# Narrow projections packed side by side, a row turned by one-row products, and a store moved to later

## The chip, the cores and the metric

The kernel runs on one core of a Trainium2 chip. The metric is device time in microseconds (us) of one execution. TensorE (PE in the rows; PEld is its weight load) multiplies, VectorE (DVE) and ScalarE (ACT) do elementwise work, GpSimd (POOL) a few small operations, and SyncE (SP) issues most transfers.

## The reference, cut to what matters

The model has two layers over 1024 tokens of width 1024. The change touches the start of layer 0 and its three small projections:

```python
mod = c_act @ ada_w[l] + ada_b[l]                 # (1, 1024) @ (1024, 6*1024)
sh1, sc1, g1, sh2, sc2, g2 = jnp.split(mod, 6, axis=-1)
h = modulate(rms_norm(x, norm1[l]), sh1, sc1)     # h * (1 + sc1) + sh1
...
xx = jnp.pad(h, ((0, 0), (1, 0), (0, 0)))[:, :-1] - h
xw = h + xx * mu[1]; xk = h + xx * mu[2]; xv = h + xx * mu[3]
xa = h + xx * mu[4]; xg = h + xx * mu[5]; xr = h + xx * mu[0]
r, k, v = xr @ w_rkv[0], xk @ w_rkv[1], xv @ w_rkv[2]
w = -softplus(-(w0 + tanh(xw @ w1) @ w2)) - 0.5   # w1: 1024 x 64
a = sigmoid(a0 + (xa @ a1) @ a2)                  # a1: 1024 x 64
g = sigmoid(xg @ g1) @ g2                         # g1: 1024 x 160
```

After these come a recurrent scan over the tokens (the wkv stage), an output projection, a feed-forward block, and a second layer with differential attention and another feed-forward block. All inputs are float32.

## The kernel before

Activations are held transposed: 128 features on the partitions, 512 tokens (half of the sequence) along the row. A width of 1024 is thus eight blocks, counted by k.

The kernel is written as generators that yield now and then, and `merge` and hand-written counters interleave them as the program is emitted. A scheduler then orders the instructions of each engine: it takes the ready instruction that stands earliest in the program, ready by its own model of the chip's times. Each engine runs that fixed order, and so does each queue that issues transfers. What stands earlier in the program thus tends to be issued earlier, but not always.

The start goes as follows. `tm_fetch(0)` loads the first half of x in four pieces (`xt`). `ada_pe` loads the first 2048 columns of the modulation weight in eight pieces of 1 MB (`adw`), and multiplies each with the column of activated conditioning as it lands (L260): four matmuls of one output row each, which write to PSUM partitions 0, 32, 64 and 96. `tm_load(0)` transposes x on TensorE (L353), copies each block to a tile `xs` (three buffers), and stores it in DRAM as `x_d` from ScalarE's queue (L356), where it is read much later; it also squares x for the norm (L349) and scales x (L361). When the modulation product is done, ScalarE copies its four rows to SBUF (L264), four transfers fold them into 16 rows of 128 (L267), one TensorE transpose turns these into 16 columns (L269), and L271 adds the bias: this is `mod`, the shift and the scale. `tm_norm(0)` then transposes the scaled x again (L375) and writes h, with scale and shift, alternately on VectorE (L379) and ScalarE (L377).

`tm_proj(0)` comes next. It loads w1, a1 and g1 (L399 to L401), and for each k makes three mixes of h with its shifted self, `xw`, `xa` and `xg` (each one ScalarE instruction, L388, and one VectorE instruction, L389), and multiplies: w1 (64 columns) into partitions 0 to 63 of the bank b1 (L408), a1 (64 columns) into partitions 64 to 127 of b1 (L410), the first 128 columns of g1 into b2 (L412), and its last 32 into b3 (L413). All three mixes share one tag with two buffers. The results are put through tanh (L417, L420), adjusted (L421) and stored as `lora_d` (L423). The second part of `tm_proj` is the three wide projections, 24 blocks each of 24 matmuls (L109 to L111) over mixes split in two parts (L100, L101); its buffers lie where those of the first part lay.

The generator `rest` is merged into `tm_proj(0)`: the transposes, squares and h of the second half of x, then the other modulation columns, summed on VectorE (`ada_ve`, L281 and L283) and turned into columns by products with ones (L290). `tm_proj(1)`, the same for the second half of the tokens, runs later beside the first tiles of the wkv stage.

Of the kernel before, what the change touches and what calls it, by code (L numbers as in the profile page):

```python
# [9 lines left out]
F32 = mybir.dt.float32  # L10
# [7 lines left out]
P = 128  # L18
# [67 lines left out]
class Trunk:  # L86
# [155 lines left out]
    def ada_pe(self, l, c0):  # L242

        nc, tc, A = self.nc, self.tc, self.A
        with self.pool("ad", ADB, "right") as ad:
            ws = []

            def fetch(n):
                for k in range(len(ws), min(n, NK)):
                    w = ad.tile([P, 2048], F32, tag="adw", name="adw")  # L250
                    nc.sync.dma_start(w, A["ada_w"][l][k * P:(k + 1) * P, c0:c0 + 2048])
                    ws.append(w)
            fetch(ADB)
            yield
            ps = self.pm.tile([P, HS], F32, tag="m", name="adps")
            for k in range(NK):
                fetch(k + 1)
                w = ws[k]
                for n in range(4):
                    nc.tensor.matmul(ps[32 * n:32 * n + 1, :], self.ca[:, k:k + 1], w[:, n * HS:(n + 1) * HS],  # L260
                                     start=(k == 0), stop=(k == NK - 1))
            row = ad.tile([P, HS], F32, tag="adrow", name="adrow", bufs=1)
            for n in range(4):
                nc.scalar.copy(row[32 * n:32 * n + 1, :], ps[32 * n:32 * n + 1, :])  # L264
            rt = ad.tile([16, P], F32, tag="adrt", name="adrt", bufs=1)
            for n in range(4):
                nc.sync.dma_start(rt[4 * n:4 * n + 4, :], row[32 * n:32 * n + 1, :])  # L267
            tp = self.pm.tile([P, HS], F32, tag="m", name="adtp")
            nc.tensor.transpose(tp[:, :16], rt, self.ident[:16, :16])  # L269
            q = c0 // P  # L270
            nc.vector.tensor_tensor(out=self.mod[l][:, q:q + 16], in0=tp[:, :16], in1=self.adab[l][:, q:q + 16], op=ALU.add)  # L271
# [71 lines left out]
    def tm_load(self, half, xn, nx):  # L343
# [6 lines left out]
        for k in range(NK):  # L350
            tp = self.pm.tile([P, HS], F32, tag="m", name="tp")
            for q in range(4):
                nc.tensor.transpose(tp[:, q * P:(q + 1) * P], xn[q][:, k * P:(k + 1) * P], self.ident)  # L353
            xs = nx.tile([P, HS], F32, tag="xs", name="xs", bufs=3)
            (nc.scalar.copy if k % 2 else nc.vector.tensor_copy)(xs, tp)
            nc.scalar.dma_start(self.x_d[half, k], xs)  # L356
            yield
# [25 lines left out]
    def mix(self, half, m, k, pool):  # L383
# [3 lines left out]
        xm = pool.tile([P, HS], F32, tag="xm", name="xm")  # L387
# [5 lines left out]
    def tm_proj(self, half):  # L393
        nc, tc, A = self.nc, self.tc, self.A
        with self.pool("lo") as lo, self.pool("lt", 2) as lt:
# [5 lines left out]
            nc.sync.dma_start(g1, A["a_g1"][0].rearrange("(k p) f -> p k f", p=P))  # L401
            b1 = self.pm.tile([P, HS], F32, tag="m", name="b1")
            b2 = self.pm.tile([P, HS], F32, tag="m", name="b2")
            b3 = self.pm.tile([P, HS], F32, tag="m", name="b3")
            for k in range(NK):
                f, l = k == 0, k == NK - 1
                xw = self.mix(half, 1, k, lt)
                nc.tensor.matmul(b1[0:64, :], w1[:, k, :], xw, start=f, stop=l)  # L408
                xa = self.mix(half, 4, k, lt)
                nc.tensor.matmul(b1[64:128, :], a1[:, k, :], xa, start=f, stop=l)  # L410
                xg = self.mix(half, 5, k, lt)
                nc.tensor.matmul(b2, g1[:, k, 0:128], xg, start=f, stop=l)  # L412
                nc.tensor.matmul(b3[0:32, :], g1[:, k, 128:160], xg, start=f, stop=l)  # L413
# [5 lines left out]
            for gl, b in ((r[2], b2), (r[3][0:32], b3[0:32, :])):  # L419
# [1295 lines left out]
def trunk(ctx, tc, A, out):  # L1715
# [9 lines left out]
    next(ada)  # L1725
    xn.append(t.tm_fetch(1, nx))
    drain(t.tm_load(0, xn[0], nx))
    drain(ada)
    t.gamma(0, 0)

# [16 lines left out]
    merge(t.tm_proj(0), side, NSA, False)  # L1747
# [151 lines left out]
```

## Time and profile before

| | us |
|---|---|
| three runs | 3251.70, 3259.11, 3259.45 |
| median of the runs | 3259.11 |
| the profiled execution's own time | 3252.99 |
| its span in the trace | 3251.2 |
| TensorE's mean granted clock in it | 0.952 of full |

The profiled execution lies 6 us under the median. In the rows below, a line such as L260 is that of the kernel before. A timeline row gives the start, the busy time, the engine, the line, the operation, what it writes and reads, the number of instructions merged into the row, and in brackets how long the engine sat idle before it and what ended that. A float32 matmul shows as two MATMUL records, each with its own weight load.

### The profile page before, as it was taken

To read this page: it belongs to the slowest core of one execution; us is meant where nothing else is said; L and a number is where in the kernel's file an instruction comes from. 1 tells how busy PE (TensorE), PEld (TensorE's weight loads), DVE (VectorE), ACT (ScalarE), POOL (GpSimd) and SP (SyncE) were. 2 spreads that over 40 slices of the span, in tenths; PEclk is the share of its full clock that TensorE was granted. 3 is DMA by queue.
4 is the path that set the end of the run, shared out by engine and by line. 5 is a ranking of instruction groups with operands and counts; after the bars stand their busy time and mean duration, and the time that the engine had idled before them with its cause. 6 is when DMAs were issued, how large, how long until landed. Compare 5 with 4: busy or idle time off the path is not lost.

```text
span 3251.2 us, 53634 instructions
## 1 busy us (share of the span) xinstructions
PE 2984.1 (92%) x21607; PEld 2400.7 (74%) x21607; DVE 2154.7 (66%) x3824; ACT 1231.3 (38%) x2189; POOL 95.1 (3%) x74
## 2 busy tenths in 40 slices
PE   5998888988899989999999789899899999999997
PEld 2574667877677767888887678778677888888885
DVE  2656877657787766777778486876667555555555
ACT  3544555565555443222223243444333212222123
POOL 0000000110000000000000000000000000000000
PEclk7999989988899999999999899999899999999998
DMA  7363334344333366455443544545552111111111
GB/s 245 114 207 112 110 106 136 103 117 136 114 118 106 101 194 209 141 171 156 141 123 127 162 122 125 151 134 155 143 192 71 52 46 41 58 52 46 39 46 52
DMA packets 441403, 387.86 MB, mean 119 GB/s; under 512 B 42832, under 2 KB 369856, under 8 KB 440130
## 3 DMA queue, kind: packets, MB, share of 16 engines
q1 hardware_dynamic: 438850, 380.23, 38.8%
q8 instruction: 170, 2.79, 0.4%
q10 hardware_dynamic: 2304, 4.20, 0.3%
q14 instruction: 79, 0.65, 0.1%
HBM read 298.74 MB, written 83.49 MB: 118 GB/s over the span
## 4 chain that ended last, share of the span: by engine, by line
PE 57%; DVE 9%; issue 5%; DMA 2%; ACT 2%; POOL 0%; SPq 0%; DVEq 0%; POOLq 0%; ACTq 0%
PE u L109 9%; PE u L111 9%; PE u L110 9%; PE d L109 5%; PE d L111 5%; PE d L110 5%; PE ps L109 3%; PE ps L110 3%; PE ps L111 3%; PE sc L1577 1%; PE tp L1504 1%; PE sc L1578 1%; DVE mx L1582 1%; DVE pd L1596 1%; DMA wraw<-in_ffn_w_up_dram 1%
## 5 line engine op out<-in xcount | busy, mean ns | idle before, releaser
L109 PE MATMUL u<-h,whl 128*128 128x512 f32 x1408 | 562.8, 400 | 5.3 <-ACT whl L163 3.8
L110 PE MATMUL u<-h,whl 128*128 128x512 f32 x1408 | 554.4, 394 | 2.4 <-DVE whl L164 2.4
L111 PE MATMUL u<-h,whl 128*128 128x512 f32 x1408 | 553.5, 393 | 1.3 <-DVE h L1129 1.3
L1172 DVE SCALAR_TENSOR_TENSOR x<-d,mod,x 128x512 f32<-128x512 f32 x352 | 261.9, 749 | 180.9 <-PE d L111 180.8
L109 PEld LDWEIGHTS u<-h,whl 128*128 128x128 f32 x1408 | 266.5, 189 | 64.9 <-ACT whl L163 4.0
L111 PEld LDWEIGHTS u<-h,whl 128*128 128x128 f32 x1408 | 266.0, 189 | 64.0 <-DVE h L1129 4.3
L110 PEld LDWEIGHTS u<-h,whl 128*128 128x128 f32 x1408 | 266.6, 189 | 57.7 <-DVE whl L164 2.9
L100 ACT CAST whl<-raw 128x1024 fp32r<-128x1024 f32 x140 | 144.0, 1043 | 434.0 <-PE d L111 420.6
L1084 DVE SCALAR_TENSOR_TENSOR a<-u,cwc,a 128x511 f32<-128x511 f32 (+1 forms) x132 | 122.0, 924 | 260.5 <-ACT a L1083 259.9
L109 PE MATMUL d<-hid,whl 128*128 128x512 f32 x704 | 280.2, 398 | 8.7 <-ACT hid L100 6.0
L110 PE MATMUL d<-hid,whl 128*128 128x512 f32 x704 | 277.3, 394 | 0.0
L1083 ACT ACTIVATE a<-u,cwc 128x512 f32<-128x512 f32 (+1 forms) x132 | 121.6, 921 | 407.6 <-PE u L111 407.4
L111 PE MATMUL d<-hid,whl 128*128 128x512 f32 x704 | 275.8, 394 | 0.0
L163 ACT CAST whl<-wraw 128x512 fp32r<-128x512 f32 x232 | 142.7, 618 | 198.0 <-PE ps L111 93.1
L164 DVE TENSOR_TENSOR whl<-wraw,whl 128x512 fp32r<-128x512 f32 x232 | 158.0, 685 | 61.6 <-ACT whl L163 59.2
L101 DVE TENSOR_TENSOR whl<-raw,whl 128x1024 fp32r<-128x1024 f32 x140 | 169.0, 1218 | 3.4 <-ACT whl L100 2.8
L109 PE MATMUL ps<-xh,whl 128*128 128x512 f32 x384 | 161.6, 423 | 8.3 <-ACT xh L100 7.5
L109 PEld LDWEIGHTS d<-hid,whl 128*128 128x128 f32 x704 | 133.4, 189 | 45.0 <-ACT hid L100 9.6
L110 PE MATMUL ps<-xh,whl 128*128 128x512 f32 x384 | 155.1, 405 | 4.7 <-DVE whl L164 4.7
L111 PE MATMUL ps<-xl,whl 128*128 128x512 f32 x384 | 155.0, 405 | 4.0 <-DVE xl L101 4.0
L111 PEld LDWEIGHTS d<-hid,whl 128*128 128x128 f32 x704 | 133.3, 189 | 30.0 <-DVE hid L101 1.7
L110 PEld LDWEIGHTS d<-hid,whl 128*128 128x128 f32 x704 | 133.4, 189 | 27.1
(279 smaller groups left out, 5859.5 us busy)
## 6 DMA issues: line engine op xcount, KB each, us to landing
raw<-in_ffn_w_up_dram SPq DMA_DIRECT2D x88, 512.0 KB
wraw<-in_a_w_rkv_dram SPq DMA_DIRECT2D x96, 256.0 KB
agw<-in_ada_w_dram SPq DMA_DIRECT2D x96, 256.0 KB
wraw<-in_ffn_w_up_dram SPq DMA_DIRECT2D x88, 256.0 KB
raw<-in_ffn_w_down_dram SPq DMA_DIRECT2D x44, 512.0 KB
agw<-in_ada_w_dram SPq DMA_DIRECT2D x128, 128.0 KB
rkv_d<-st SPq DMA_DIRECT2D x48, 256.0 KB
wraw<-in_a_w_o_dram SPq DMA_DIRECT2D x48, 256.0 KB
```

What stands on the lines that cost most here:

```text
L100: nc.scalar.copy(h, src)
L101: nc.vector.tensor_tensor(out=l, in0=src, in1=h.bitcast(F32), op=ALU.subtract)
L109: nc.tensor.matmul(ps, wh, xh, start=first, stop=False)
L110: nc.tensor.matmul(ps, wl, xh, start=False, stop=False)
L111: nc.tensor.matmul(ps, wh, xl, start=False, stop=last)
L163: nc.scalar.copy(wt[:, 0], raw)
L164: self.low().tensor_tensor(out=wt[:, 1], in0=raw, in1=wt[:, 0].bitcast(F32), op=ALU.subtract)
L1083: nc.scalar.activation(a, u, AF.Identity, bias=c[3], scale=c[2])
L1084: nc.vector.scalar_tensor_tensor(out=a[:, 1:], in0=u[:, :n - 1], scalar=c[1], in1=a[:, 1:], op0=ALU.mult, op1=ALU.add)
L1172: nc.vector.scalar_tensor_tensor(out=xs, in0=ps, scalar=gate[:, j:j + 1], in1=xs, op0=ALU.mult, op1=ALU.add)
L1504: nc.tensor.transpose(tp[:, i * P:(i + 1) * P], p[:, (b0 + i) * P:(b0 + i + 1) * P], self.ident)
L1577: nc.tensor.matmul(sc[:, bl], H.q[c][:, tsl], H.ks[c][:, bl], start=True, stop=False)
```

## The change

Three things are edited.

In `ada_pe`, the four rows are copied to one row of 2048 on one partition, two copies by ScalarE and two by VectorE. The four transfers and the transpose are gone; in their place 16 matmuls, each with a 1x128 piece of the row as weights and a single one as the moving operand, write the 16 columns.

In `tm_load`, `xs` has eight buffers instead of three. For the first half the stores to `x_d` are collected, and issued from SyncE's queue after the modulation is done; the second half stores as before.

In `tm_proj`, the three weight loads of the first half are emitted before the second half of x is fetched. The mixes have a tag each, with three buffers; `xw` and `xa` are both made ahead of the two matmuls that use them. The 32-column product is held until two mixes `xg` are there, and is then issued as two matmuls into partitions 0 to 31 and 32 to 63 of b3; at the end a copy and an addition sum the two parts. This holds for both halves of the tokens.

```diff
@@ ada_pe
-            row = ad.tile([P, HS], F32, tag="adrow", name="adrow", bufs=1)
+            row = ad.tile([1, 2048], F32, tag="adrow", name="adrow", bufs=1)
             for n in range(4):
-                nc.scalar.copy(row[32 * n:32 * n + 1, :], ps[32 * n:32 * n + 1, :])
-            rt = ad.tile([16, P], F32, tag="adrt", name="adrt", bufs=1)
-            for n in range(4):
-                nc.sync.dma_start(rt[4 * n:4 * n + 4, :], row[32 * n:32 * n + 1, :])
+                (nc.vector.tensor_copy if n % 2 else nc.scalar.copy)(row[0:1, n * HS:(n + 1) * HS], ps[32 * n:32 * n + 1, :])
+
             tp = self.pm.tile([P, HS], F32, tag="m", name="adtp")
-            nc.tensor.transpose(tp[:, :16], rt, self.ident[:16, :16])
+            for n in range(16):
+                nc.tensor.matmul(tp[:, n:n + 1], row[0:1, n * P:(n + 1) * P], self.cst[0:1, C_ONE:C_ONE + 1], start=True, stop=True)
@@ tm_load
-            xs = nx.tile([P, HS], F32, tag="xs", name="xs", bufs=3)
+            xs = nx.tile([P, HS], F32, tag="xs", name="xs", bufs=NK)
             (nc.scalar.copy if k % 2 else nc.vector.tensor_copy)(xs, tp)
-            nc.scalar.dma_start(self.x_d[half, k], xs)
+            if half:
+                nc.scalar.dma_start(self.x_d[half, k], xs)
+            else:
+                self.xs0.append(xs)
@@ mix
-    def mix(self, half, m, k, pool):
+    def mix(self, half, m, k, pool, tag="xm"):
-        xm = pool.tile([P, HS], F32, tag="xm", name="xm")
+        xm = pool.tile([P, HS], F32, tag=tag, name="xm")
@@ tm_proj
-        with self.pool("lo") as lo, self.pool("lt", 2) as lt:
+        with self.pool("lo") as lo, self.pool("lt", 3) as lt:
...
+            if half == 0:
+                yield
+            last = None
             for k in range(NK):
                 f, l = k == 0, k == NK - 1
-                xw = self.mix(half, 1, k, lt)
+                xw, xa = self.mix(half, 1, k, lt, "xw"), self.mix(half, 4, k, lt, "xa")
+
                 nc.tensor.matmul(b1[0:64, :], w1[:, k, :], xw, start=f, stop=l)
-                xa = self.mix(half, 4, k, lt)
                 nc.tensor.matmul(b1[64:128, :], a1[:, k, :], xa, start=f, stop=l)
-                xg = self.mix(half, 5, k, lt)
+                xg = self.mix(half, 5, k, lt, "xg")
                 nc.tensor.matmul(b2, g1[:, k, 0:128], xg, start=f, stop=l)
-                nc.tensor.matmul(b3[0:32, :], g1[:, k, 128:160], xg, start=f, stop=l)
+                if k % 2 == 0:
+                    last = xg
+                else:
+
+                    for i, x in enumerate((last, xg)):
+                        nc.tensor.matmul(b3[32 * i:32 * i + 32, :], g1[:, k - 1 + i, 128:160], x, start=k == 1, stop=l)
...
-            for gl, b in ((r[2], b2), (r[3][0:32], b3[0:32, :])):
+            nc.scalar.copy(r[3][0:32], b3[32:64, :])
+            nc.vector.tensor_tensor(out=r[3][0:32], in0=b3[0:32, :], in1=r[3][0:32], op=ALU.add)
+            for gl, b in ((r[2], b2), (r[3][0:32], r[3][0:32])):
@@ trunk
     next(ada)
+    proj = t.tm_proj(0)
+    next(proj)
     xn.append(t.tm_fetch(1, nx))
+    t.xs0 = []
     drain(t.tm_load(0, xn[0], nx))
     drain(ada)
     t.gamma(0, 0)
+    for k in range(NK):
+        t.nc.sync.dma_start(t.x_d[0, k], t.xs0[k])
...
-    merge(t.tm_proj(0), side, NSA, False)
+    merge(proj, side, NSA, False)
```

## Rows read from the trace of the kernel before

**Rows 1.** Page, part 1: busy us (share) xinstructions of each engine.

```profile
PE 2984.1 (92%) x21607; PEld 2400.7 (74%) x21607; DVE 2154.7 (66%) x3824; ACT 1231.3 (38%) x2189; POOL 95.1 (3%) x74
```

**Rows 2.** Windows: PE, PEld, DVE, ACT, POOL busy (x); PEclk, DMA share, GB/s.

```profile
14.00:45.00 31.00, 16.25 (x83) 5.38 (x87) 5.57 (x9) 3.50 (x6) 1.01 (x1) 0.75 0.94 351
...
47.00:54.00 7.00, 2.15 (x9) 1.75 (x9) 0.25 (x2) 6.50 (x12) 0.03 (x1) 0.50 0.75 207
...
75.00:103.00 28.00, 24.28 (x48) 4.76 (x46) 16.11 (x26) 13.41 (x19) 0.00 (x0) 1.00 0.16 47
...
125.00:276.00 151.00, 139.88 (x656) 113.20 (x655) 84.06 (x150) 63.72 (x112) 0.00 (x0) 0.98 0.61 188
276.00:335.00 59.00, 49.72 (x220) 20.70 (x220) 42.05 (x82) 30.09 (x54) 4.44 (x4) 0.91 0.26 71
```

**Rows 3.** Timeline, 14 to 47 us: TensorE waiting for x and for the modulation weight.

```profile
14.23 0.91 PE L353 MATMUL tp<-cst,xt 128*128 128x128 f32 x3 [0.38 <-DMA xt<-in_x_dram]
...
44.65 1.89 PE L260 MATMUL adps<-adw,dv 128*1 128x512 f32 x8 [1.05 <-DMA adw<-in_ada_w_dram]
```

**Rows 4.** Waits of SyncE's queue, 0 to 120 us: total us, times, longest.

```profile
SPq L251 <- DMA x_d<-xs: 20.7, 4, 10.2
```

**Rows 5.** Timeline, 46 to 54 us: the modulation row is turned.

```profile
46.60 2.38 ACT L264 COPY adrow<-adps 1x512 f32<-1x512 f32 x4 [10.62 <-PE adps L260]
47.20 2.73 SPq L267 DMA_DIRECT2D adrt<-adrow  x4
...
51.10 0.26 PE L269 MATMUL adtp<-cst,adrt 16*128 16x16 f32 x1 [4.57 <-DMA adrt<-adrow]
...
53.73 0.17 DVE L306 TENSOR_SCALAR rs<-ss 128x4 f32<-128x4 f32 x1 [18.40 <-ACT junk L349]
53.80 0.17 DVE L271 TENSOR_TENSOR mod<-adtp,cols 128x16 f32<-128x16 f32 x1
```

**Rows 6.** Timeline, weight loads of 128 float32 columns, two places.

```profile
69.33 0.50 PEld L412 LDWEIGHTS b<-xm,g 128*128 128x128 f32 x2 [1.61 <-issue]
...
265.00 0.64 PEld L290 LDWEIGHTS agps<-cst,agacc 128*128 128x128 f32 x4
...
265.56 0.19 PEld L109 LDWEIGHTS ps<-xh,whl 128*128 128x128 f32 x1
```

**Rows 7.** Timeline, TensorE, one k of the narrow projections.

```profile
94.35 1.07 PE L408 MATMUL b<-xm,w 128*64 128x512 f32 x2
96.02 1.07 PE L410 MATMUL b<-xm,a 128*64 128x512 f32 x2 [0.60 <-DVE xm L389]
97.03 1.12 PE L412 MATMUL b<-xm,g 128*128 128x512 f32 x2
98.08 1.04 PE L413 MATMUL b<-xm,g 128*32 128x512 f32 x2
99.06 0.64 PE L408 MATMUL b<-xm,w 128*64 128x512 f32 x1
```

**Rows 8.** Timeline, TensorE, the first narrow products of the first half.

```profile
60.20 0.64 PE L408 MATMUL b<-xm,w 128*64 128x512 f32 x1
60.21 0.64 PE L410 MATMUL b<-xm,a 128*64 128x512 f32 x1
...
60.69 0.59 PE L410 MATMUL b<-xm,a 128*64 128x512 f32 x1
```

**Rows 9.** Groups by line, 63 to 103 us: busy, mean ns, idle before and releasers.

```profile
L389 DVE SCALAR_TENSOR_TENSOR xm<-h,cols,xm 128x512 f32<-128x512 f32 x22 | 16.4, 750 | 18.0 <-ACT xm L388 18.0
L388 ACT ACTIVATE xm<-h,dv 128x512 f32<-128x512 f32 x20 | 14.4, 722 | 22.0 <-PE b L413 9.8 <-PE b L410 7.6 <-PE b L408 4.6
```

**Rows 10.** Timeline, 103 to 110 us: from the last narrow product to the wide ones.

```profile
103.67 1.04 PE L413 MATMUL b<-xm,g 128*32 128x512 f32 x2
...
108.41 1.14 ACT L100 CAST xh<-xm 128x512 fp32r<-128x512 f32 x2 [2.48 <-DMA lora_d<-lr]
...
109.08 0.80 PE L109 MATMUL ps<-xh,whl 128*128 128x512 f32 x1 [3.78 <-ACT xh L100]
```

## The prediction

> **What bounds the kernel now.** I read the page first. TensorE is busy for 92% of the span, VectorE for 66%, ScalarE for 38% [rows 1]; a change at the start pays where TensorE stands still. The windows show where that is. From 14 to 45 us the transfer engines are the bound: their share is 0.94 at 351 GB/s, and TensorE is busy for 16 of 31 us [rows 2]. From 47 to 54 us TensorE is nearly empty, at half its clock. From 75 to 103 us it looks busy, 24.3 of 28 us, but VectorE and ScalarE have room there. From 125 to 276 us it is busy for 139.9 of 151 us at 0.98 of its clock: whatever arrives there earlier moves the end by about as much. From 276 to 335 us, where the second half's narrow projections run beside the first wkv tile, TensorE has 49.7 of 59 us and VectorE 42.1.
>
> The timeline then names the waits. TensorE waits for the modulation weight up to 44.65, and ends with it at 46.54 [rows 3]. SyncE's queue, which loads that weight, spent 20.7 us in waits that ended with an `x_d` store [rows 4]. Turning the row takes from 46.60 to 51.36, and `mod` is added only at 53.80, since VectorE had the second half's L306 ahead of it in its order, which waited for that half's squares [rows 5]. In the narrow projections one k takes 4.71 us from start to start [rows 7], and the groups by line say why: the mixes on VectorE waited 18.0 us for ScalarE's part, and ScalarE's part 22.0 us for TensorE to free one of two buffers [rows 9]. The engines run in lockstep.
>
> **The stores moved.** Eight stores of 256 KB, 2.10 MB, leave the stretch in which the weight arrives. At 351 GB/s [rows 2] that is 6.0 us. From 14 to 45 us 10.9 MB moved: 8.39 of weight, 2.10 of stores, some 0.4 of x's second half, which now stands behind the narrow weights as well; so the upper bound is 7 us, the lower 0 (if other transfers fill the place). I take 6.5, since the queue itself waited on these stores [rows 4]: the last product ends near 40.0 instead of 46.54. The stores now stand on SyncE ahead of the wraw loads, 6 us of transfer at the same rate, and nothing needs these loads before the wide products, over 30 us later. If that cover were gone they would cost their 6 us. The extra `xs` buffers let the transposes run on, which alone gains nothing: TensorE would then only wait longer for the weight.
>
> **The turn.** Removed: 46.60 to 51.36, 4.8 us [rows 5]. Added: four copies, two and two beside each other; at 0.6 us each (2.38 for four) the first pair costs 0.6 and the second hides behind the products. Then 16 products, 32 records with a weight load each. The nearest loads of 128 float32 columns take 0.14 us each at the full clock (265.00 to 265.56 for four) and 0.25 each near half (0.50 for two) [rows 6]: 4.5 to 8.0 us. The clock around the turn is 0.50 [rows 2], but products issued back to back may raise it; I take 6.4, in all 7.0, so the turn by itself loses 2.2 us (0.3 to 3.8).
>
> That a one-row weight is no cheaper than a full one is also what the Trainium skill says ("TensorE: Matmul & The Clock Gate", LDWEIGHTS): the load's time follows the columns, not the contraction rows. By its figure of 107 ns for 128 columns the 32 loads would be an estimated 3.4 us, and the turn 4.0; no row here has a one-row load of 128 columns.
>
> **When `mod` is ready.** 40.0 + 7.0 + 0.2 = 47.2. The second half of x now comes behind 1.18 MB of narrow weights: 11.7 MB from 14.2 on [rows 3] at 351 GB/s is 47.4, and with the last square 48.7. If VectorE keeps L306 ahead, `mod` is near 49.2; if not, 47.2. I take 48.2 against 53.97 before: 5.8 us gained (2 to 9).
>
> **The narrow projections.** Before, the stage lasted from 53.97 to 104.71 [rows 5, 10], 50.7 us: 6.2 to the first product at 60.20 [rows 8], 37.7 for eight k at 4.71, and 6.8 of slow first steps, where the first g product came only at 69.33 [rows 6] and matmuls ran near half clock. After, TensorE per k: the w and a products ran beside each other wherever both mixes were ready: 60.20 and 60.21, all four records over by 61.28, 1.08 us instead of 2.14 [rows 8]. With g at 1.05 and the 32-column product at 0.98 per two k [rows 7] that is 2.55 us per k. VectorE needs 3 x 0.75 = 2.25, ScalarE 3 x 0.72 = 2.17 [rows 9]. VectorE also has some 5 us of other work in this stretch (16.1 us busy from 75 to 103, of which six k of mixes are 13.4 [rows 2, 9], and as much again before), so VectorE sets it: 18.0 + 5.4 = 23.4, 2.9 per k. The lead-in of 6.2 stays, I leave 3 us for first steps at low clock: 6.2 + 23.2 + 3.0 + 0.6 for the last pair = 33.0 against 50.7, 17.7 us gained. Bounds: 4.8 if only the 0.6 us wait per k goes [rows 7]; 21 if TensorE's 2.55 is reached.
>
> The Trainium skill bears on the packing too: by "TensorE: Matmul & The Clock Gate", Part 3, three column tiles gave 2.38 times, not 3. At that efficiency two tiles would take an estimated 1.35 us instead of 1.08, some 2 us over a half; the rows here show no such loss, and they decide.
>
> **The end of the stage.** A copy (0.6, as L264's) and an addition (at most 0.75, as a mix) stand ahead of the last tanh, in a chain that ends in the `lora_d` store, whose landing frees the buffers of the first wide product [rows 10]. TensorE waits there: 1.3 us lost. First half: 5.8 + 17.7 - 1.3 = 22.2.
>
> **The second half.** Before, the four products of a k occupy 4.11 us of TensorE without the wait [rows 7]; after, 2.55: 12.5 us less over eight k. How much of it shortens 276 to 335 us depends on what else is there: VectorE's 42 us stay [rows 2], and the wkv tile is a chain of its own. From 0 to 12.5; I take 7.
>
> **Sum.** 22.2 + 7 = 29.2 off 3252.99 is 3223.8. That execution lies 6 us under the median of the runs, and the new runs may scatter likewise; I add 2: **3226**.
>
> **Rivals.** *The second half gives nothing* (0.18): VectorE and the wkv chain set that stretch. For it: the 42 us and the waits between VectorE and ScalarE. Against: TensorE has 84% of the stretch. 3226 + 7 = 3233.
>
> *Packing does not happen midway* (0.07): the rows show it only at a first k; later the second product might wait for its own mix, or for its weights behind the 128-column product. Then only the waits go: 5.8 + 4.8 + 3.8 (first steps) - 1.3 = 13, and 2 in the second half: 3240.
>
> *The order on VectorE and ScalarE* (0.05): the mixes, no longer paced by buffers, are mingled with other ready work so that a k takes 4 us. 23.2 becomes 32, half of the second gain goes: 3226 + 9 + 4 = 3239.
>
> *TensorE's clock* (0.04), the other side. Packed, the products leave the array idle between k, and it may fall to 1.2 GHz for both narrow stages. For it: 0.50 at 47 to 54 us, where it was little used. Against: 0.91 from 276 to 335 us [rows 2]. At the lower level records take about twice as long: 2 x 2.55 = 5.1 per k against 4.71, 3 us lost in the first half; in the second, 37 us of records (49.7 - 12.5) become some 68 in place of 59, 9 us lost; with the turn at its dearest, -5.8 + 1.6 + 1.3 + 3 + 9 = 9 us slower, 3262 to 3265. It decides if the granted clock of 276 to 335 us falls under about 0.55. The same page of the Trainium skill (HAM oscillation) says that idle gaps between bursts bring the clock down; the 0.50 agrees, and by that rule this would be the result if the gaps were long enough.
>
> **How the numbers follow.** The forecast has 0.66. Its own range is 3212 (the gains at 9, 21 and 12.5 less 1.3, no scatter) to 3237. The first three rivals end by 3243, the fourth is left out below 3262: range 3209 to 3243. 0.3%, about what a measurement can tell from no change, is 10 us. Faster holds the forecast and nearly all of the first three rivals, less scatter: 0.92; same 0.06; slower, the dear end of the clock rival, 0.02.
>
> **What would show it.** Right: the last modulation product ending near 40 us, `mod` near 48, the last narrow product near 81, the first wide one near 87 instead of 109.08, w and a records starting within 0.05 us of each other, under 3 us per k, and the wkv stage's start earlier still. Wrong: the weight landing after 43 us in spite of the moved stores; L306 or the squares, waiting for x, ahead of `mod` by more than 3 us; ScalarE or VectorE waiting within the k; granted clock under 0.7 in the narrow stages; or a gain at 87 us that is given back before 350 us.

## The result, and the profile after

| | before | after |
|---|---|---|
| runs | 5 | 5 |
| median, us | 3259.45 | 3232.16 |
| lowest to highest, us | 3251.70 to 3270.45 | 3227.92 to 3241.04 |
| profiled execution, its span, us | 3252.99, 3251.2 | 3236.66, 3234.9 |

The ratio of the times is 0.9908 (95% interval 0.9892 to 0.9924): 0.9% faster, 27 us between the medians. The forecast of 3226 lies 6 us under the new median, and the range holds it. The sum of the prediction was 29 us; one of its terms was off by a factor of two, and that the total came so near is in part luck: gains that were larger than forecast stand against losses far behind the edit that were not foreseen.

In the kernel after, the lines move: w1's product is L414, a1's L415, g1's 128 columns L417, its 32 columns L423, the mixes L390 (ScalarE) and L391 (VectorE), the one-row products L268, the bias addition L270, the `lora_d` stores L435, the late `x_d` stores L1746.

The whole looks as before on the page's first part, since the edit touches a tenth of the span:

```profile
PE 2977.3 (92%) x21638; PEld 2412.0 (75%) x21638; DVE 2154.9 (67%) x3828; ACT 1226.5 (38%) x2189; POOL 95.0 (3%) x74
```

The windows of the kernel after show the stages (columns as in [rows 2]):

```profile
14.00:38.00 24.00, 16.42 (x92) 5.83 (x90) 5.67 (x10) 4.01 (x8) 2.49 (x2) 0.86 1.02 382
38.00:46.00 8.00, 8.00 (x39) 7.64 (x39) 1.56 (x5) 0.58 (x1) 0.00 (x0) 0.52 1.04 385
51.00:75.00 24.00, 24.00 (x65) 5.02 (x64) 17.19 (x27) 20.37 (x35) 1.01 (x1) 1.00 0.31 78
75.00:82.00 7.00, 1.22 (x8) 0.74 (x8) 3.92 (x7) 4.46 (x9) 0.00 (x0) 0.80 0.90 262
...
254.00:293.00 39.00, 34.70 (x151) 15.44 (x152) 33.60 (x71) 24.38 (x47) 3.97 (x2) 0.97 0.33 92
```

From 14 to 38 us the transfers now run at 382 GB/s; before, they had 351 from 14 to 45 us. In the narrow stage, 51 to 75, TensorE is busy for all 24.00 us: here it, not VectorE, sets the stage. From 75 to 82 it stands nearly still. The granted clock is 1.00 in the first half's narrow stage and 0.97 in the second's, so the rival about the clock is out.

The timeline of the turn, kernel after:

```profile
36.02 1.04 PE L260 MATMUL adps<-adw,dv 128*1 128x512 f32 x8 [0.91 <-DMA adw<-in_ada_w_dram]
37.12 0.57 ACT L264 COPY adrow<-adps 1x512 f32<-1x512 f32 x1 [15.14 <-PE adps L260]
37.73 0.68 DVE L264 COPY adrow<-adps 1x512 f32<-1x512 f32 x1 [13.80 <-ACT adrow L264]
37.75 1.43 PE L268 MATMUL adtp<-cst,adrow 1*128 1x1 f32 x8 [0.69 <-ACT adrow L264]
38.27 7.13 SPq L1746 DMA_DIRECT2D x_d<-xs  x7
38.44 0.58 ACT L264 COPY adrow<-adps 1x512 f32<-1x512 f32 x1 [0.75 <-DVE adrow L264]
39.05 0.69 DVE L264 COPY adrow<-adps 1x512 f32<-1x512 f32 x1 [0.64 <-ACT adrow L264]
...
40.15 5.28 PE L268 MATMUL adtp<-cst,adrow 1*128 1x1 f32 x24
...
45.47 0.17 DVE L270 TENSOR_TENSOR mod<-adtp,cols 128x16 f32<-128x16 f32 x1 [5.72 <-PE adtp L268]
```

The last modulation product ends at 37.06 (46.54 in [rows 3]). The four copies go strictly one after the other, each waiting for the one before it on the other engine: from 37.12 to 39.74. The 24 last records take 0.22 us each; the granted clock is 0.52 from 38 to 46 us. `mod` starts at 45.47 instead of 53.80 [rows 5], and it waited for the products alone: neither L306's work nor x's squares held it.

TensorE's timeline inside the narrow stage, kernel after:

```profile
61.68 1.13 PE L417 MATMUL b<-xm,g 128*128 128x512 f32 x2
62.73 1.05 PE L423 MATMUL b<-xm,g 128*32 128x512 f32 x2
63.71 0.64 PE L414 MATMUL b<-xm,w 128*64 128x512 f32 x1
63.72 0.64 PE L415 MATMUL b<-xm,a 128*64 128x512 f32 x1
64.19 0.59 PE L414 MATMUL b<-xm,w 128*64 128x512 f32 x1
64.19 0.59 PE L415 MATMUL b<-xm,a 128*64 128x512 f32 x1
64.72 1.13 PE L417 MATMUL b<-xm,g 128*128 128x512 f32 x2
...
67.84 1.05 PE L423 MATMUL b<-xm,g 128*32 128x512 f32 x4
```

w and a start 0.01 us apart and make room for g 1.01 us later. But the two 32-column products of a pair mostly stand apart: at 62.73 there are two records, one product, alone for 0.98 us. The only pair side by side in this half is the row with x4 at 67.84; the scheduler moves the first product of each other pair up to where it is ready. So eight k take from 50.61 to 74.98, 3.05 us per k, where [rows 7] had 4.71.

The groups by line, 51 to 75 us, kernel after, beside [rows 9]:

```profile
L391 DVE SCALAR_TENSOR_TENSOR xm<-h,cols,xm 128x512 f32<-128x512 f32 x25 | 17.2, 747 | 4.1 <-ACT xm L390 4.1
L390 ACT ACTIVATE xm<-h,dv 128x512 f32<-128x512 f32 x24 | 15.4, 710 | 1.4 <-PE b L423 1.4
```

The lockstep is gone: ScalarE's wait for buffers falls from 22.0 to 1.4 us, VectorE's for ScalarE from 18.0 to 4.1.

Then the end of the stage, kernel after, beside [rows 10]:

```profile
73.93 1.05 PE L423 MATMUL b<-xm,g 128*32 128x512 f32 x2
...
75.01 0.58 ACT L429 COPY lr<-b 32x512 f32<-32x512 f32 x1 [0.80 <-PE b L423]
...
75.62 0.68 DVE L430 TENSOR_TENSOR lr<-b,lr 32x512 f32<-32x512 f32 x1 [3.06 <-ACT lr L429]
...
76.61 0.62 ACT L432 ACTIVATE lr<-lr 32x512 f32<-32x512 f32 x1
...
77.25 1.19 SPq L435 DMA_DIRECT2D lora_d<-lr  x2
...
81.36 1.14 ACT L100 CAST xh<-xm 128x512 fp32r<-128x512 f32 x2 [2.37 <-DMA lora_d<-lr]
82.03 0.79 PE L109 MATMUL ps<-xh,whl 128*128 128x512 f32 x1 [5.12 <-ACT xh L100]
```

The first wide product starts at 82.03, 27.05 us earlier. The second half's narrow stage shortens as well. These are the records of w1's product there, with the first and the last start, in the kernel after:

```profile
L414 PE MATMUL b<-xm,w x16: 592/618/643, 252.0 to 284.0; 128*64 128x512 f32 x16
```

and in the kernel before:

```profile
L408 PE MATMUL b<-xm,w x16: 592/592/963, 277.7 to 328.3; 128*64 128x512 f32 x16
```

From its first narrow product to the end of its last that stage takes 35.0 us (251.98 to 286.98) instead of 56.8 (277.72 to 334.54). Of these 21.8 us only part arrives: the first state product of the second half in the wkv stage moves from 392.7 to 357.9, 34.8 us, 7.8 more than the first wide product. Far behind, at the down projection, 25.2 of the 34.8 are left. A large piece of the loss shows at one product of the feed-forward block, `u`. In the kernel after:

```profile
1254.86 0.77 PE L109 MATMUL u<-h,whl 128*128 128x512 f32 x1 [9.75 <-DVE mu L1139]
```

In the kernel before, the same place:

```profile
1278.24 0.80 PE L109 MATMUL u<-h,whl 128*128 128x512 f32 x1 [1.60 <-ACT h L1128]
```

This is the start of the first layer's feed-forward block, second half, a thousand microseconds behind the edit, in lines that the diff does not touch. It is taken up below.

### The profile page after: what moved, and what is told of

Its sections match the earlier page's. It is cut to its first block, busy times and chain, and to the rows that moved or that the text cites. A ratio compares the mean times of both kernels' runs of the same rounds, so it can differ in the third digit from the quotient of the medians.

```text
span 3234.9 us, 53676 instructions
## 1 busy us (share of the span) xinstructions
PE 2977.3 (92%) x21638; PEld 2412.0 (75%) x21638; DVE 2154.9 (67%) x3828; ACT 1226.5 (38%) x2189; POOL 95.0 (3%) x74
## 4 chain that ended last, share of the span: by engine, by line
PE 65%; DVE 15%; issue 9%; DMA 6%; ACT 4%; POOL 1%; SPq 0%; DVEq 0%; POOLq 0%; ACTq 0%
PE u L109 8%; PE u L110 8%; PE u L111 8%; PE d L109 5%; PE d L111 5%; PE d L110 5%; PE ps L109 4%; PE ps L111 4%; PE ps L110 4%; DMA agw<-in_ada_w_dram 2%; DVE whl L164 1%; PE wp L713 1%; PE sc L1589 1%; DVE agacc L282 1%; PE tp L1516 1%
## 5 line engine op out<-in xcount | busy, mean ns | idle before, releaser
L109 PE MATMUL ps<-xh,whl 128*128 128x512 f32 x384 | 163.3, 426 | 11.3 <-ACT xh L100 10.5
L109 PEld LDWEIGHTS d<-hid,whl 128*128 128x128 f32 x704 | 133.5, 190 | 46.4 <-ACT hid L100 9.3
```

The lines of the kernel that those rows point to most:

```text
L109: nc.tensor.matmul(ps, wh, xh, start=first, stop=False)
```

## The experiments

Each kernel is the one after with the edit shown, unless said otherwise. Times are medians; the ratio is that to the kernel before on the same chip, with its 95% interval. The last two have one run each. The landmarks are starts in the traces, in us: the bias addition `mod`, the first wide product, the first state product of the second wkv part (L753 before), the first addition of the down projection (L1172 before), and the last scaling of the output (L1240 before).

| kernel | us | ratio | mod | wide | wkv | down | output |
|---|---|---|---|---|---|---|---|
| before | 3259.45 | 1 | 53.8 | 109.08 | 392.7 | 1305.5 | 3245.9 |
| after | 3232.16 | 0.9908 [0.9892, 0.9924] | 45.5 | 82.03 | 357.9 | 1280.3 | 3229.7 |
| stores_early | 3249.40 | 0.9962 [0.9948, 0.9977] | 55.8 | 93.34 | 369.8 | 1298.8 | 3249.3 |
| stores_early_8buf | 3245.28 | 0.9949 [0.9931, 0.9967] | 52.3 | 89.62 | 367.1 | 1282.2 | 3230.1 |
| turn_by_transfers | 3234.25 | 0.9910 [0.9897, 0.9924] | 46.4 | 83.99 | 366.3 | 1284.7 | 3231.4 |
| weights_late | 3240.34 | 0.9929 [0.9907, 0.9952] | 44.0 | 83.26 | 359.5 | 1281.8 | 3235.0 |
| buffers_alone | 3248.32 | 0.9961 [0.9946, 0.9977] | 44.7 | 86.75 | 374.1 | 1297.5 | 3237.7 |
| first_half_only | 3240.77 | 0.9935 [0.9923, 0.9947] | 46.2 | 83.71 | 367.9 | 1293.6 | 3233.9 |
| no_pairs | 3230.67 | 0.9910 [0.9891, 0.9928] | 46.2 | 83.91 | 358.0 | 1278.8 | 3224.3 |
| pairs_together | 3233.67 | 0.9923 [0.9905, 0.9942] | 45.3 | 80.40 | 354.5 | 1280.3 | 3227.3 |
| lr_apart | 3231.93 | 0.9907 [0.9891, 0.9924] | 44.6 | 79.69 | 353.7 | 1270.4 | 3220.5 |
| combined | 3218.58 | 0.9866 [0.9851, 0.9881] | 41.3 | 73.93 | 346.8 | 1272.3 | 3212.4 |
| before_again | 3253.37 | | 52.8 | 107.12 | 393.2 | 1306.3 | 3246.3 |
| after_again | 3230.30 | | 46.4 | 83.42 | 357.1 | 1276.1 | 3223.4 |

Two traces of one program differ by up to about 2 us at the early landmarks and up to 6 at the late ones (before and before_again, after and after_again). Smaller differences between kernels are read from the rows, not from the table; a difference of two kernels at `mod` or at the first wide product can be off by some 2 us.

**stores_early** and **stores_early_8buf**: the stores go out at once, with three buffers `xs` and with eight.

```diff
-            xs = nx.tile([P, HS], F32, tag="xs", name="xs", bufs=NK)
+            xs = nx.tile([P, HS], F32, tag="xs", name="xs", bufs=3)   # stores_early alone
-            if half:
-                nc.scalar.dma_start(self.x_d[half, k], xs)
-            else:
-                self.xs0.append(xs)
+            nc.scalar.dma_start(self.x_d[half, k], xs)
...
-    for k in range(NK):
-        t.nc.sync.dma_start(t.x_d[0, k], t.xs0[k])
```

> The changed kernel with the stores of the first half's transposed input put back: from ScalarE's queue at once, three buffers. If these stores are what held the modulation weight back, its last product ends near 46.5 us again instead of 37.1, the first wide product moves from 82.0 to about 91, and the whole is some 9 us slower than the changed kernel (some 18 faster than the kernel before, 0.994 to 0.995 of it). If the weight came earlier for another reason (the order of SyncE's queue, the early narrow weights), both stay within 2 us of the changed kernel.

> The changed kernel with the first half's stores issued at once from ScalarE's queue again, but with the eight buffers kept. If it is the stores' traffic that held the weight back, this run is like the one with three buffers: last modulation product near 46 us, some 9 us slower than the changed kernel. If it was the wait of the transposes for a free buffer, it is like the changed kernel, the last product near 37 us.

The last group of modulation products starts at 45.08 with three buffers, at 41.59 with eight, and at 36.02 in the kernel after. So the move is worth more than its bytes. The transfer windows, 14 to 36 us, first stores_early (columns as in [rows 2]):

```profile
14.00:36.00 22.00, 11.79 (x63) 5.28 (x63) 5.58 (x9) 3.50 (x6) 1.96 (x2) 0.84 0.93 349
```

stores_early_8buf:

```profile
14.00:36.00 22.00, 12.28 (x63) 4.15 (x63) 5.49 (x9) 3.48 (x7) 1.97 (x2) 0.75 1.01 401
```

and SyncE's waits from 0 to 120 us, in stores_early

```profile
SPq L251 <- DMA x_d<-xs: 18.5, 4, 10.9
```

and in stores_early_8buf:

```profile
SPq L251 <- DMA x_d<-xs: 7.1, 2, 5.2
```

With three buffers the transfers run at 349 GB/s and the loading queue waits 18.5 us behind stores; with eight, 401 GB/s and 7.1 us; in the kernel after no such wait is left, and the same window has 396 GB/s. The start of the last group thus moves by 3.5 us for the buffers, which keep the loading queue moving, and by 5.6 us for the 2.1 MB of stores (at 401 GB/s they take 5.2); two traces of one program differ by up to 1.0 us there (44.65 and 43.64 before, 36.02 and 35.68 after). The eight records of that group take 1.04 us in the kernel after, at a granted clock of 1.00, and 1.88 in both of these, at 0.50. That is no gain of the move: in the second trace of the kernel after they take 1.89 us, at 0.50 too. At the first wide product the two kernels are 11.3 and 7.6 us behind the kernel after, in the medians of the whole 17.2 and 13.1; runs of stores_early_8buf spread from 3231.6 to 3255.1, so the rest is not assigned.

**turn_by_transfers**: the row is turned as before, by four transfers and one transpose.

```diff
-                (nc.vector.tensor_copy if n % 2 else nc.scalar.copy)(row[0:1, n * HS:(n + 1) * HS], ps[32 * n:32 * n + 1, :])
+                nc.scalar.copy(row[32 * n:32 * n + 1, :], ps[32 * n:32 * n + 1, :])
+            rt = ad.tile([16, P], F32, tag="adrt", name="adrt", bufs=1)
+            for n in range(4):
+                nc.sync.dma_start(rt[4 * n:4 * n + 4, :], row[32 * n:32 * n + 1, :])
...
-            for n in range(16):
-                nc.tensor.matmul(tp[:, n:n + 1], row[0:1, n * P:(n + 1) * P], self.cst[0:1, C_ONE:C_ONE + 1], start=True, stop=True)
+            nc.tensor.transpose(tp[:, :16], rt, self.ident[:16, :16])
```

> The changed kernel with the row turned by four transfers and one transpose again. If the sixteen one-row products are only dearer than the transfers, as the durations say (8.3 us from the last modulation product to the last of them, against 4.8 before), mod is ready near 42 us instead of 45.6, and the first wide product near 78.5: some 3.5 us faster than the changed kernel. If the transfers now have to wait behind the narrow weights and the second half of x, 3.3 MB that are under way at that time (8.6 us at 382 GB/s), mod comes at 46 to 50 us and the kernel is 0 to 4 us slower.

Timeline, 36 to 48 us, TensorE and SyncE's queue:

```profile
45.80 0.26 PE L269 MATMUL adtp<-cst,adrt 16*128 16x16 f32 x1 [8.76 <-DMA adrt<-adrow]
```
```profile
38.28 2.75 SPq L267 DMA_DIRECT2D adrt<-adrow  x4
```

The prediction set the 4.8 us of [rows 5] against the products and let the turn lose 2.2 us. The transfers no longer cost 4.8: they are issued from 38.28 to 41.03, behind the narrow weights and x's second half that the same change put ahead of them, and the transpose starts only at 45.80, 4.8 us after the last issue (1.2 us in [rows 5]). So the turn by products, 8.4 us from 37.06 to 45.43, loses nothing beside it; 0.9 us of difference in `mod` is within the scatter, and so are the whole times.

**weights_late**: the narrow weights are fetched after x's second half, as before.

```diff
-    proj = t.tm_proj(0)
-    next(proj)
     xn.append(t.tm_fetch(1, nx))
...
+    proj = t.tm_proj(0)
+    next(proj)
     merge(proj, side, NSA, False)
```

> The changed kernel with the narrow weights loaded where they were, after the norm of the first half. If the early load matters, g1 lands after the stores of the transposed input and the loads ahead of it, the first g product comes near 60 us instead of 52.6, and the first wide product some 5 to 8 us later than 82. If the load has cover, both kernels agree within 2 us; the second half of x would then land 3 us earlier, which nothing waits for.

`mod` is 1.5 us earlier, but the first narrow product waits for its weight, as TensorE's timeline shows:

```profile
52.35 1.04 PE L414 MATMUL b<-xm,w 128*64 128x512 f32 x2 [1.96 <-DMA w<-in_a_w_dram]
```

It is 1.7 us later than the 50.61 of the kernel after, and the first wide product 1.2 later. The early fetch is worth a microsecond or two at most; in the whole time the intervals overlap. In this run the first eight one-row products of the turn fell into a stretch with a granted clock of 1.00 (37.70 to 38.80 us):

```profile
37.73 1.05 PE L268 MATMUL adtp<-cst,adrow 1*128 1x1 f32 x8 [0.70 <-ACT adrow L264]
```

That is 0.13 us for each record, against 0.22 at the lower level.

**buffers_alone** and **first_half_only**: in both the second half's narrow part is as before. In first_half_only the first half is that of the change. In buffers_alone its mixes have the new tags and buffers, but no two products stand beside each other: a1 writes partitions 0 to 63 of a bank of its own, and the 32 columns are issued for each k.

```diff
+            if half:
+                ...   (loop of the kernel before, two buffers)
                 nc.tensor.matmul(b1[0:64, :], w1[:, k, :], xw, start=f, stop=l)
-                nc.tensor.matmul(b1[64:128, :], a1[:, k, :], xa, start=f, stop=l)
+                nc.tensor.matmul(b4[0:64, :], a1[:, k, :], xa, start=f, stop=l)      # buffers_alone
...
-                if k % 2 == 0:
...
+                nc.tensor.matmul(b3[0:32, :], g1[:, k, 128:160], xg, start=f, stop=l)  # buffers_alone
```

> As the run with the new projections in the first half only, but there the products stand one after the other: the a product goes to its own bank at partitions 0 to 63, and the 32-column product is made for every k, so that no two narrow products have different columns of the array; the three tags with three buffers stay. If TensorE sets the stage, a k takes 4.1 us, the eight take 33 us, and the first wide product comes 9 to 12 us later than in that run (91 to 94 us). If the mixes on VectorE set it, as the prediction had it, a k stays near 2.9 us and the first wide product is within 3 us.

> The changed kernel with the second half's narrow projections as before (one tag, two buffers, one product after the other). The first wide product stays at 82 us. If the second half's gain lasts, the wkv chain's first state product comes some 8 us later than in the changed kernel (358 us there) and the whole is 8 us slower, 0.994 of the kernel before. If the wkv stage gives that gain back, the whole is within 3 us of the changed kernel.

TensorE's timeline in buffers_alone:

```profile
61.74 1.07 PE L415 MATMUL b<-xm,w 128*64 128x512 f32 x2
62.65 1.02 PE L416 MATMUL b<-xm,a 128*64 128x512 f32 x2
63.61 1.12 PE L418 MATMUL b<-xm,g 128*128 128x512 f32 x2
64.66 1.05 PE L419 MATMUL b<-xm,g 128*32 128x512 f32 x2
65.64 1.07 PE L415 MATMUL b<-xm,w 128*64 128x512 f32 x2
```

No row waits, and one k takes 3.90 us: the buffers alone bring 4.71 down by the waits, and what is left is TensorE's own time, w 0.91, a 0.96, g 1.05, 32 columns 0.98 from start to start. Packed, w and a take 1.01 together instead of 1.87, 1.85 times as fast. The narrow stage takes 31.7 us here (49.98 to 81.67) and 24.5 in first_half_only (52.27 to 76.72). At the first wide product, where 9 to 12 us were expected, 3.0 us of those 7.2 are left: first_half_only began 2.3 us later, and its end, with the copy and the addition, took 1.9 us longer (76.72 to 83.71 against 81.67 to 86.75). At the wkv landmark buffers_alone is 6.2 us behind, and its median is 7.6 us longer, with intervals that just touch.

first_half_only against after gives the second half's part: the wkv landmark is at 367.9 instead of 357.9, and the whole is 8.6 us longer, with intervals that touch at 0.992. That rival (the second half gives nothing) falls. The time alone could not tell: the rival's 3233 lies nearer to the measured 3232 than the forecast.

**no_pairs** issues the 32 columns for each k, without the sum at the end; **pairs_together** ties both products of a pair behind the second k's 128-column product, so that they are issued one right after the other.

```diff
-                if k % 2 == 0:
-                    last = xg
-                else:
...
+                nc.tensor.matmul(b3[0:32, :], g1[:, k, 128:160], xg, start=f, stop=l)   # no_pairs
```
```diff
-                nc.tensor.matmul(b2, g1[:, k, 0:128], xg, start=f, stop=l)
+                gi = nc.tensor.matmul(b2, g1[:, k, 0:128], xg, start=f, stop=l)
...
+                    with tc.issue_after(gi.ins):   # pairs_together
                         for i, x in enumerate((last, xg)):
```

> The changed kernel with the 32-column product made for every k again, without pairs and without the sum at the end. In the changed kernel only one of the four pairs of the first half, and one of the second, ran side by side, so the theory gives this run one more product of 1.0 us per half and 1.3 us less at the end: within 2 us of the changed kernel. If the pairs pay as the prediction had it, 0.5 us per k, it is 4 us slower per half less 1.3, some 5 us in all.

> The changed kernel with an edge for the scheduler alone, that both products of a pair stand behind the second k's 128-column product on TensorE. If TensorE sets the narrow stage, three slots of 1.0 us go in the first half: a k takes 2.55 us, the first wide product comes near 79 us instead of 82.0, and the whole is 3 to 5 us faster. If VectorE sets it, nothing moves by more than 1 us.

Without pairs nothing is lost that can be measured (0.9910): in the change as it stands one pair in four runs side by side, and the sum costs its time.

Tied together, three of the four pairs run side by side, but the expected 3 us do not come. From the first narrow product to the end of the last the stage takes 24.1 us (50.46 to 74.56) instead of 24.4. For one thing, a mix now holds TensorE up:

```profile
68.57 1.12 PE L417 MATMUL b<-xm,g 128*128 128x512 f32 x2 [0.43 <-DVE xm L391]
```

Ahead of it VectorE itself waited for ScalarE's part of the mixes, 0.9 to 1.05 us before each of three of them, with ScalarE's squares of x's second half (L348) in between. Twice w and a start 0.3 us apart, and four transposes of x stand between the last two products. The first wide product comes at 80.40, 1.6 us earlier; 1.2 of these lie behind the last narrow product, and two traces of the kernel after differ by 1.4. The whole time shows no difference (0.9923, intervals overlap).

**lr_apart**: the first half's results are written to the two buffers of x, long free, instead of to new ones that the wide part's buffers follow.

```diff
-            r = [lo.tile([P, HS], F32, name=f"lr{i}") for i in range(4)]
+            if half == 0:
+                r = [self.xn0[i // 2][:, i % 2 * HS:(i % 2 + 1) * HS] for i in range(4)]
+            else:
+                r = [lo.tile([P, HS], F32, name=f"lr{i}") for i in range(4)]
...
-    t.xs0 = []
+    t.xs0, t.xn0 = [], xn[0]
```

> The changed kernel with the first half's narrow results put into tiles of the first half of x, which nothing reads by then, so that the first wide product's mixes need not wait for the store of these results to land. If that landing is the wait of 5.1 us ahead of the first wide product, the product comes at 77 to 78 us instead of 82.0, and the whole is some 4 us faster. If the mixes and the splits are late themselves, it comes within 1.5 us of 82.

The wait for the landing of the store goes, and another takes most of its place. Timeline of lr_apart:

```profile
79.04 0.60 ACT L163 CAST whl<-wraw 128x512 fp32r<-128x512 f32 x1
...
79.69 0.80 PE L109 MATMUL ps<-xh,whl 128*128 128x512 f32 x1 [3.59 <-ACT whl L163]
```

The split `xh` is now ready at 75.9, but ScalarE splits the weight only at 79.04, behind other work in its fixed order. The first wide product comes 2.3 us earlier, not the 4 to 5 expected; 1.5 of these are gained behind the last narrow product (5.5 us from its end to the first wide one, instead of 7.05). The whole time shows no difference to after.

**combined**: pairs_together, lr_apart, and the row turned by 16 one-row transposes instead of 16 products.

```diff
-                nc.tensor.matmul(tp[:, n:n + 1], row[0:1, n * P:(n + 1) * P], self.cst[0:1, C_ONE:C_ONE + 1], start=True, stop=True)
+                nc.tensor.transpose(tp[:, n:n + 1], row[0:1, n * P:(n + 1) * P], self.ident[:1, :1])
```

> The changed kernel with three more edits: the narrow results in tiles of x, the pairs side by side, and the sixteen one-row products as transposes, which are one record each instead of two. If the costs add, 3 us at the turn, 3 at the pairs and 4 at the end of the stage: first wide product near 72 us, the whole some 10 us faster than the changed kernel, 0.988 of the kernel before. If the stage is bound elsewhere (VectorE, ScalarE), 78 us and 4 us faster.

TensorE's timeline of combined:

```profile
38.28 0.58 PE L268 MATMUL adtp<-cst,adrow 1*128 1x1 f32 x4 [0.70 <-ACT adrow L264]
...
39.84 1.44 PE L268 MATMUL adtp<-cst,adrow 1*128 1x1 f32 x12
...
53.65 0.64 PE L414 MATMUL b<-xm,w 128*64 128x512 f32 x1
...
57.78 1.05 PE L423 MATMUL b<-xm,g 128*32 128x512 f32 x4
58.77 0.64 PE L414 MATMUL b<-xm,w 128*64 128x512 f32 x1
...
65.39 1.12 PE L417 MATMUL b<-xm,g 128*128 128x512 f32 x2 [0.43 <-DVE xm L391]
...
73.93 0.50 PE L109 MATMUL ps<-xh,whl 128*128 128x512 f32 x1 [1.96 <-ACT xh L100]
```

The transposes are 16 records of 0.12 to 0.15 us, not 32 of 0.18 to 0.22, and `mod` comes at 41.31. Three of the four pairs run side by side, and from 53.65 on two k take 5.12 us (53.65 to 58.77) and the next two 5.11: the 2.55 per k of the prediction. From 65 us on VectorE holds TensorE up as in pairs_together, and all eight k take 23.8 us (47.61 to 71.39), against 24.4 in after. The first wide product is 8.1 us earlier than in after. `mod` is 4.2 us earlier, the first narrow product 3.0, the end of the last 3.6; the other 4.5 come behind it (2.5 us to the first wide product instead of 7.05). This is the best version: 0.9866 of before against 0.9908, intervals apart, some 14 us faster than after. At the down landmark it is 8.0 us ahead of the first trace of after and 3.8 of the second; the rest comes behind that.

**before_again** and **after_again** run both kernels a second time, to tell what of the shrinking distance behind 358 us belongs to the program.

> The kernel before once more, for a second trace. Against the first trace of before, the changed kernel is 34.5 us ahead at the end of the first layer's wkv output (the first sum of squares after it), 25 at the first down projection, and 16 at the end. If these 18 us are the spread between executions (the first profiled one lay 6 us under its median), this trace reaches the same places 5 to 10 us later than the first trace of before. If the changed program itself gives them back in later stages, it reaches them within 2 us of the first trace.

> The changed kernel once more, for a second trace. Up to the first wide product (82.0 us) both traces should agree within 1 us, and from the last wkv tile to the end they should differ by as much as the two traces of before do, 5 to 10 us, if the later differences are spread between executions; if they belong to the program, within 2 us.

The wait of 9.7 to 9.8 us at `u` is in both traces of the kernel after and in those of all ten variants; both traces of the kernel before have 1.6. So no single edit that was taken back here removes it. From the last wkv state product to the first addition of the down projection the kernels before take 147.1 and 145.6 us, the kernels after 152.5 and 153.0: 5 to 7 us given back by the program. More is lost behind it: from the down landmark to the output the kernels before take 1940.4 and 1940.0 us, the kernels after 1949.4 and 1947.3, which is 7 to 9 us more, while two traces of one program differ by 2.1 at most. buffers_alone, first_half_only and combined take 1940.1 to 1940.3 there, as long as the kernel before, the other variants 1945.5 to 1953.2. Which edit makes the difference, and in which place, stays open.

The semaphores in the two traces say more of `u`. Before, its first product waits for ScalarE alone, and every third one for VectorE, each for its own block of h. After, the first one waits at once for VectorE, TensorE and ScalarE.

In the trace after it starts at 1254.86, when the eighth `mu` has been made (1253.97 to 1254.71), though h's first block was ready at 1247.4. The eighth `mu` is the last reader of R, which TensorE wrote to PSUM; a bank that `u` takes over from R would need just these waits. That the order of the PSUM buffers came out otherwise is argued from the waits and was not tried.

## Why the prediction was nearly right

The gains came at the places that the prediction named. Three of its reasons were wrong (what the buffers do, what the turn is compared with, what sets the narrow stage), and most sizes were off. By its terms (us; first trace after against first trace before, and second against second):

| step | predicted | first traces | second traces |
|---|---|---|---|
| last modulation product earlier | 6.5 | 9.5 | 8.0 |
| turn, from there to `mod` | 7.0 | 8.4 | 8.8 |
| `mod` earlier | 5.8 | 8.3 | 6.4 |
| narrow stage shorter | 17.7 | 21.4 | 19.9 |
| end of the stage longer | 1.3 | 2.7 | 2.6 |
| first wide product earlier | 22.2 | 27.05 | 23.7 |
| second half | 7 | 7.8 at the wkv landmark | 12.3 there |
| lost from the last wkv state product to the down landmark | 0 | 5.4 | 7.4 |
| lost from the down landmark on | 0 | 9.0 | 7.3 |

**The stores.** "The extra `xs` buffers let the transposes run on, which alone gains nothing" was wrong. The rows of SyncE's waits [rows 4] named stores as what held the loading queue; the prediction read that as traffic alone and bounded it by bytes. 3.5 us came from the buffers, and the bound of 7 was broken in both pairs of traces.

**The turn.** The copies are not two and two beside each other, they alternate, 2.6 us in all, though the first products overlap them. The records were sized well: 6.7 us in place of 6.4 (1.43 + 5.28), at a granted clock of 0.52. The estimate of 3.4 us for these loads, from the Trainium skill ("TensorE: Matmul & The Clock Gate", LDWEIGHTS), is half of that; most of the difference goes with the clock, since at 1.00 eight records took 1.05 us in weights_late, an estimated 4.2 for all 32. More wrong was what the products were compared with: the transfers would have been queued behind the moved weights, at 9.0 us (37.04 to 46.06), so the loss of 2.2 did not exist.

**When `mod` is ready.** Neither L306 nor the squares held it. The 1 us left for them was not needed.

**The narrow stage.** "so VectorE sets it" was wrong for the kernel after: TensorE was busy without a gap. The prediction had TensorE at 2.55 per k (the terms as written, 1.08 + 1.05 + 0.49, add up to 2.62; 2.56 is what combined has from start to start) and took the pairs as issued together; they were not, and TensorE needed 3.05. The mixes stand close behind, though: with the pairs tied, eight k take 24.1 and 23.8 us, 3.0 per k and not 2.55, near the 2.9 that the prediction gave VectorE. Both errors nearly cancel per k (2.9 against 3.05); the gain came from the first steps, which ran at full clock (1.00 from 51 us on), where 3 us had been left for a low one, and from a lead-in of 5.0 us from `mod` to the first product instead of 6.2. The bounds of packing hold: 1.85 times for w and a, and 0.98 us for two 32-column products where one alone takes 0.98. The Trainium skill's 2.38 for three tiles ("TensorE: Matmul & The Clock Gate", Part 3) is a loss of a fifth; here it is a thirteenth for w and a, and none for the 32 columns.

**The end of the stage.** The copy and the addition were counted, 1.3, and with ScalarE's turn in between they cost 1.5: the last tanh ends 2.25 us after the last product (74.98 to 77.23), 0.76 before. The rest is the landing: from that tanh to the split that waits for it 4.1 us instead of 2.9, in a stretch where the transfer engines' share is 0.90 (0.66 before, from 104 to 109 us).

**The second half.** Its gain was bounded by 12.5 us, TensorE's records alone; its narrow stage shortened by 21.8, since the waits between the engines went too, and 7.8 to 12.3 of that reached the wkv landmark. That 7 came near is luck.

**The rivals.** The second half's gain, 7.8 at the wkv landmark and 8.6 in the whole, rules out the first. Packing did happen midway in the first half, for w and a from the second k on, for the 32 columns in one pair of four; that part of the rival came true, at 0.5 us per k. The order on VectorE did not bind in the kernel after, and TensorE's clock rose instead of falling.

**What was missing** are the losses behind 358 us. The prediction looked for gains given back before 350 us. At the wkv landmark the kernel after is 34.8 and 36.0 us ahead, 6 to 7 more than the 29.2 of the sum; between the medians 27 are left. Without the longer wait at `u`, 5 to 7 us, the time would have come out at an estimated 3226. Why that wait came, and what was lost behind the down landmark, was argued or left open, not shown.

## What to carry to other kernels

A wait row that names a store ahead of a load says more than the bytes of the store: with few buffers and a shared queue the load is late by its place, too, so count both. Two products side by side are only so when they are issued together; where a scheduler may pull one up, tie them, and look in the trace for the merged row. Then look at what stands next: here a late mix, w and a starting apart, and transposes took up nearly all that the tied pairs freed. After an early gain, compare landmarks along the whole span: a program that is scheduled anew can lose part of it a thousand microseconds later, in lines nobody touched.

## What was not expected of the hardware

A one-row float32 product of 128 weight columns is two records, of 0.22 us each at a granted clock of 0.52 and of 0.13 at 1.00 (weights_late); the transpose of the same piece is one record of 0.12 at 0.50 (38.0 to 41.3 us of combined). TensorE was busy for all 8.00 us from 38 to 46 at that lower level, and had 1.00 from 51 to 75, where it was busy for all 24.00 too. Loading went from 349 to 401 GB/s by more buffers for a store that shares the transfer engines, with the DMA share going from 0.93 to 1.01.
